# Query and key projections: the input's high and low parts moved through TensorE together

## The chip, the core and the metric

The kernel runs on one core of a Trainium2 chip. The metric is the time of one execution on the device in microseconds. Before the change it is 883.79 us, the median of three runs (883.66 to 884.83).

The core's engines work side by side, each through its own queue in order: TensorE (PE) multiplies matrices and writes its sums to PSUM, a memory of 8 banks of 128 partitions by 512 fp32; VectorE (DVE) and ScalarE (ACT) do elementwise work and can read PSUM; GpSimd (POOL) does elementwise work in SBUF; SyncE (SP) issues the loads of weights.

## The reference

A decoder trunk of two layers over 256 tokens of 1024 features, all in fp32. Each layer normalises its input, projects it, runs three attention mixers beside each other, gates and adds them, and then a feed-forward network. The parts around the change:

```python
    h = _rms_norm(x, attn_norm)
    proj = h @ w_in
    aq, ak, av, bq, bk, bv, c_q, c_kv_pe, gates = jnp.split(proj, offsets, axis=-1)
    ...
    y_a = _diff_attention(aq, ak, av, lam, lam_init, slopes_a, diff_norm) @ w_branch_a
    y_b = _dilated_attention(bq, bk, bv, slopes_b) @ w_branch_b
    y_c = _mla(c_q, c_kv_pe, mla_q_norm, mla_w_uq, mla_kv_norm, mla_w_ukv, pos) @ w_branch_c
```

The change is in the computation of `aq`, `ak`, `bq` and `bk`, 512 features each, in both layers.

## The kernel before

**Numbers in two parts.** The matmuls take numbers of a short format (`F32R`). Each fp32 operand is therefore split: ACT writes the rounded high part (`hi_of`, L222), DVE the remainder, the low part (`lo_of`, L225). A product is three matmuls, high by high, high by low and low by high, added in PSUM (`mm3`, L212).

**Weights.** A fixed list (`PLAN`) orders the pieces of all weights, each up to 128 x 1024. SP loads a piece into one of five `raw` tiles, ACT and DVE split it into one of five pairs `whi`/`wlo`, and `take` (L255) hands it out, after it has split the piece that lies three further on. A piece of a query or key projection holds four blocks of 128 inputs for 256 features, so one projection of 256 features takes two pieces.

**The input.** The normalised input lies transposed in tiles `fr`, as `self.xs`: for each of eight blocks of 128 features one run of 512 columns, the 256 tokens' high parts and then their low parts. The division by the root mean square comes after the projection: `Rb` (L421) is a row of one factor per token, repeated in all partitions and for two feature blocks.

**The projections.** `qk_proj` (L505) is called twice in a layer, for the first mixer (`stacked`) and for the second. A call makes four projections, j = 0 and 1 the queries, 2 and 3 the keys, each 256 features by 256 tokens. `pair_job` (L263) puts a projection into one bank: two halves of 128 features, each 256 columns, three matmuls per input block and half, with the weights standing and the input moving. DVE then reads the bank once, times `Rb` (queries also times the scale, L514; keys L516), into an `f` tile; the bank is returned, and the `f` tile is split again for the scores (`stacked` L491, `split` L232, `key_pair` L486).

**Banks.** Four banks form the ring `banks` for projections and the feed-forward network, four the ring `att` for attention. A bank that is returned goes to the end of its ring. While the latent projections of the third mixer wait for their factor, they hold two banks of the first ring. After the first `qk_proj` comes `mla_up` (L548), the query up-projection, with four banks: per block of 128 tokens two, 384 columns each.

**The order of work.** The generator `dense` (L455) yields after each piece; the attention's stages are called in between, 16 heads of three kinds (four of the first mixer, eight latent heads, four of the second) with fixed lags (L919 to L936). The program is built by a planner that simulates the engines' times (L1147) and sets the order of every engine's queue from that; so the order on the chip is fixed, and not always that of the source. In the first layer POOL also makes the mask tables (`tables`, L326) and in both it rotates the latent keys and queries (`rope`, L594).

Of the kernel before, what the change touches and what calls it, by code (L numbers as in the profile page):

```python
# [14 lines left out]
AF = mybir.ActivationFunctionType  # L15
ALU = mybir.AluOpType
# [163 lines left out]
def split_rows(t):  # L180
    return t.rearrange("p (c t) -> p c t", c=2)


class Build:
# [76 lines left out]
        return [(self.whi[j][:, k * nc_:(k + 1) * nc_], self.wlo[j][:, k * nc_:(k + 1) * nc_]) for k in range(nk)]  # L261

    def pair_job(self, ps, x, nk):  # L263
        k = 0
        while k < nk:
            for wh, wl in self.take():
                for c in range(2):
                    s = slice(c * 128, c * 128 + 128)
                    self.mm3(ps[:, c * 256:c * 256 + 256], wh[:, s], wl[:, s], x[k][:, 0:256], x[k][:, 256:512],
                             k == 0 and c == 0, k == nk - 1)  # L270
                k += 1
            if k < nk:
                yield
# [231 lines left out]
    def qk_proj(self, q, k, scale, stacked):  # L505
        nc = self.nc
        for j in range(4):
            bank = self.banks.get()
            yield from self.pair_job(bank, self.xs, KT)
            ps = split_rows(bank)  # L510
            t = self.f.get()
            tv = split_rows(t)
            if j < 2:
                nc.vector.scalar_tensor_tensor(out=tv, in0=ps, scalar=-scale, in1=self.Rb, op0=ALU.mult, op1=ALU.mult)  # L514
            else:
                nc.vector.tensor_tensor(out=tv, in0=ps, in1=self.Rb, op=ALU.mult)  # L516
            self.banks.put(bank)
            if stacked:
                (q if j < 2 else k).append(self.stacked(t, j < 2, j))
            elif j < 2:  # L520
                hi, lo = self.fr.get(), self.fr.get()
                self.split(hi, lo, t)
                q.append((hi, lo))
            else:
                k.append(self.key_pair(tv))
            self.f.put(t)
            yield
# [624 lines left out]
```

## Time and profile before

| | us |
|---|---|
| Median of three runs | 883.79 |
| The profiled execution | 883.18 |
| Its span, first to last instruction | 881.4 |
| PE busy | 873.6 |
| DVE busy | 591.1 |
| ACT busy | 502.2 |
| POOL busy | 71.4 |

The profile is one execution. Busy time is the time in which an engine has an instruction under way; matmuls overlap, so a busy PE may still have its instructions spaced out. In a row of a timeline the first two numbers are the start and the length in us from the span's start; `out<-in` are tiles, `xN` merges N like instructions, and a bracket at the end tells how long the engine was idle before it and who ended that. For a matmul the tile named first after the arrow is the one that moves.

### The profile page before, as it was taken

How to read it: one execution, taken by the hardware profiler on the slowest of the kernel's cores; microseconds unless marked ns; L12 is line 12 of the kernel's file. 1: busy time of each engine (PE TensorE's matmuls, PEld its weight loads, DVE VectorE, ACT ScalarE, POOL GpSimd, SP SyncE). 2: the span in 40 equal slices, each digit the busy share in tenths (PEclk: the TensorE clock that was granted, in tenths of full speed). 3: DMA queues.
4: the chain of work that ended last, by engine and by line, in shares of the span. 5: the costliest groups of instructions: out<-in, count | busy, mean ns of one | idle time of the engine just before them, and what ended most of it. 6: DMA issues, size and time to landing. Idle time of an engine off the chain costs nothing.

```text
span 881.4 us, 12736 instructions
## 1 busy us (share of the span) xinstructions
PE 873.6 (99%) x4710; PEld 759.5 (86%) x4710; DVE 591.1 (67%) x990; ACT 502.2 (57%) x852; POOL 71.4 (8%) x95
## 2 busy tenths in 40 slices
PE   9999999999999999999999999999999999999997
PEld 9989988888888888888899899888888888888886
DVE  5988878665666655555467888786556666656444
ACT  7797777644454444444376867775454644444332
POOL 1940310000000000000011303100000000000000
PEclk9999999999999999999999999999999999999999
DMA  9756444456656665656475553444555556655541
GB/s 340 245 170 209 128 141 160 146 169 193 187 167 197 187 190 182 182 186 191 127 226 174 172 168 128 151 145 159 180 189 182 167 193 202 203 190 180 181 141 49
DMA packets 45423, 155.92 MB, mean 177 GB/s; under 512 B 5168, under 2 KB 6192, under 8 KB 45360
## 3 DMA queue, kind: packets, MB, share of 16 engines
q1 hardware_dynamic: 44928, 154.55, 55.0%
q8 instruction: 37, 0.61, 0.3%
q10 hardware_dynamic: 432, 0.55, 0.2%
q14 instruction: 26, 0.21, 0.1%
HBM read 154.03 MB, written 1.05 MB: 176 GB/s over the span
## 4 chain that ended last, share of the span: by engine, by line
PE 97%; POOL 1%; issue 1%; DVE 0%; ACT 0%; POOLq 0%
PE bank L210 87%; PE att L210 6%; PE att L445 2%; PE att L719 1%; PE att L767 0%; PE att L768 0%; PE att L769 0%; POOL f L602 0%; PE att L693 0%; PE att L851 0%; POOL f L604 0%; POOL f L603 0%; POOL q_tm L605 0%; DVE x_tm L1043 0%; ACT x_tm L1058 0%
## 5 line engine op out<-in xcount | busy, mean ns | idle before, releaser
L210 PE MATMUL bank<-whi,fr 128*128 128x512 f32 (+1 forms) x2032 | 631.1, 387 | 0.0
L228 DVE TENSOR_TENSOR wlo<-raw,whi 128x1024 fp32r<-128x1024 f32 (+2 forms) x294 | 353.9, 1206 | 250.8 <-ACT whi L223 250.1
L223 ACT ACTIVATE whi<-raw 128x1024 fp32r<-128x1024 f32 (+2 forms) x294 | 305.0, 1041 | 305.8 <-PE bank L210 246.0
L210 PEld LDWEIGHTS bank<-whi,fr 128*128 128x128 f32 x2032 | 379.8, 188 | 71.5 <-ACT whi L223 0.2
L210 PE MATMUL bank<-wlo,fr 128*128 128x512 f32 (+1 forms) x1016 | 390.1, 386 | 0.0
L210 PEld LDWEIGHTS bank<-wlo,fr 128*128 128x128 f32 x1016 | 191.0, 188 | 35.5 <-DVE wlo L228 0.3
L210 PE MATMUL bank<-fr,whi 128*128 128x256 f32 x512 | 94.6, 285 | 0.0
L210 PEld LDWEIGHTS bank<-fr,whi 128*128 128x128 f32 x512 | 80.0, 192 | 0.2
L210 PE MATMUL bank<-fr,wlo 128*128 128x256 f32 x256 | 73.0, 285 | 0.0
L210 PEld LDWEIGHTS bank<-fr,wlo 128*128 128x128 f32 x256 | 49.0, 192 | 0.0
L372 POOL TENSOR_TENSOR r<-small,mhalf 128x2 f32<-128x2 f32 x4 | 2.8, 708 | 477.5 <-DVE small L398 462.6
L759 ACT ACTIVATE s<-s,small 128x256 f32<-128x256 f32 (+1 forms) x80 | 35.8, 455 | 1.2 <-DVE small L757 0.8
L372 POOL TENSOR_TENSOR small<-small,mhalf 128x2 f32<-128x2 f32 (+1 forms) x12 | 10.0, 831 | 280.5 <-DVE small L1047 178.5
L223 ACT ACTIVATE fr<-att 128x512 fp32r<-128x512 f32 (+2 forms) x54 | 28.3, 559 | 4.1 <-PE att L719 2.3
L210 PE MATMUL att<-whi,fr 128*128 128x288 f32 (+1 forms) x108 | 29.9, 290 | 0.0
L228 DVE TENSOR_TENSOR fr<-att,fr 128x512 fp32r<-128x512 f32 (+2 forms) x46 | 28.2, 634 | 0.1
L223 ACT ACTIVATE fr<-f 64x512 fp32r<-64x512 f32 (+2 forms) x40 | 23.3, 583 | 6.7 <-DVE f L516 5.4
L210 PE MATMUL att<-fr,fr 96*128 96x256 f32 (+3 forms) x152 | 26.0, 277 | 0.0
L210 PEld LDWEIGHTS att<-fr,fr 96*128 96x128 f32 (+1 forms) x152 | 22.7, 190 | 0.6
L615 ACT ACTIVATE f<-bank,rh 128x512 f32<-128x512 f32 x24 | 16.3, 689 | 11.7 <-PE bank L210 11.7
L972 ACT ACTIVATE f<-bank,rh 128x512 f32<-128x512 f32 (+1 forms) x24 | 15.6, 654 | 12.2 <-PE bank L210 12.2
L210 PEld LDWEIGHTS att<-whi,fr 128*128 128x128 f32 x108 | 20.4, 191 | 0.1
(134 smaller groups left out, 636.0 us busy)
## 6 DMA issues: line engine op xcount, KB each, us to landing
raw<-w SPq DMA_DIRECT2D x272, 512.0 KB, 3.6
raw<-w SPq DMA_DIRECT2D x16, 336.0 KB, 3.2
raw<-w SPq DMA_DIRECT2D x6, 384.0 KB, 3.6
x_tm<-xt SPq DMA_DIRECT2D x2, 512.0 KB, 6.4
f<-x SPq DMA_DIRECT2D x3, 256.0 KB, 5.2
f<-fnorm SPq DMA_DIRECT2D x2, 256.0 KB, 4.2
out<-x_tm ACTq DMA_DIRECT2D x2, 256.0 KB, 2.2
f<-x SPq DMA_DIRECT2D x2, 128.0 KB, 3.1
```

What stands on the lines that cost most here:

```text
L210: self.nc.tensor.matmul(out, lhsT, rhs, start=start, stop=stop, skip_group_check=True)
L223: self.nc.scalar.activation(out=hi, in_=src, func=AF.Copy, scale=scale)
L228: self.nc.vector.tensor_tensor(out=lo, in0=src, in1=h, op=ALU.subtract)
L372: self.nc.gpsimd.tensor_tensor(out=out, in0=v, in1=self.mhalf[:, 0:v.shape[1]], op=ALU.pow)
L445: self.nc.tensor.transpose(ps[:, c, b * 128:b * 128 + 128], src[b][:, c0 + c * 128:c0 + c * 128 + 128], self.ident)
L615: nc.scalar.activation(out=t[b], in_=bank[b], func=AF.Tanh, scale=self.rh[:, b:b + 1])
L719: nc.tensor.transpose(ps[0:96, c, b * 128:b * 128 + 128], src[:, b, 2 * p + c, :], self.ident)
L759: nc.scalar.activation(out=s[:, SL[b]], in_=s[:, SL[b]], func=AF.Exp, bias=mn[:, b:b + 1], scale=-1.0, accum_out=z[:, b:b + 1])
L972: nc.scalar.activation(out=a, in_=g, func=AF.Tanh, scale=self.rh[:, b:b + 1])
```

## The change

A projection now takes two banks, one for each half of 128 features. For an input block, the high weights meet the whole run of 512 columns, so that the products with the high and with the low part lie side by side in the bank; the low weights meet the 256 high columns. On reading, ACT copies the right half of a bank to the `f` tile, with the scale for queries, DVE adds the left half to it, and POOL multiplies both halves by `Rb`.

```diff
     def pair_job(self, ps, x, nk):
...
                 for c in range(2):
                     s = slice(c * 128, c * 128 + 128)
-                    self.mm3(ps[:, c * 256:c * 256 + 256], wh[:, s], wl[:, s], x[k][:, 0:256], x[k][:, 256:512],
-                             k == 0 and c == 0, k == nk - 1)
+                    self.mm(ps[c], wh[:, s], x[k], k == 0, False)
+                    self.mm(ps[c][:, 0:256], wl[:, s], x[k][:, 0:256], False, k == nk - 1)
                 k += 1
...
     def qk_proj(self, q, k, scale, stacked):
         nc = self.nc
         for j in range(4):
-            bank = self.banks.get()
+            bank = [self.banks.get() for _ in range(2)]
             yield from self.pair_job(bank, self.xs, KT)
-            ps = split_rows(bank)
             t = self.f.get()
             tv = split_rows(t)
-            if j < 2:
-                nc.vector.scalar_tensor_tensor(out=tv, in0=ps, scalar=-scale, in1=self.Rb, op0=ALU.mult, op1=ALU.mult)
-            else:
-                nc.vector.tensor_tensor(out=tv, in0=ps, in1=self.Rb, op=ALU.mult)
-            self.banks.put(bank)
+            sign = -scale if j < 2 else 1.0
+            for c in range(2):
+                nc.scalar.activation(out=tv[:, c], in_=bank[c][:, 256:512], func=AF.Copy, scale=sign)
+                nc.vector.scalar_tensor_tensor(out=tv[:, c], in0=bank[c][:, 0:256], scalar=sign, in1=tv[:, c],
+                                               op0=ALU.mult, op1=ALU.add)
+            self.banks.put(*bank)
+            nc.gpsimd.tensor_tensor(out=tv, in0=tv, in1=self.Rb, op=ALU.mult)
```

## Rows read from the trace of the kernel before

**Rows 1.** The page's head and busy table: us, share of the span, instructions.
```profile
span 881.4 us, 12736 instructions
...
PE 873.6 (99%) x4710; PEld 759.5 (86%) x4710; DVE 591.1 (67%) x990; ACT 502.2 (57%) x852; POOL 71.4 (8%) x95
```

**Rows 2.** The page's chain that ended last, shares of the span by engine.
```profile
PE 97%; POOL 1%; issue 1%; DVE 0%; ACT 0%; POOLq 0%
```

**Rows 3.** The page's groups, PE: busy us, mean ns, idle before.
```profile
L210 PE MATMUL bank<-fr,whi 128*128 128x256 f32 x512 | 94.6, 285 | 0.0
...
L210 PE MATMUL bank<-fr,wlo 128*128 128x256 f32 x256 | 73.0, 285 | 0.0
```

**Rows 4.** Pieces of the chain in order of time: start us, us, what.
```profile
82.35 2.87 PE bank L210 x24
...
283.29 21.79 PE bank L210 x96
```

**Rows 5.** Groups by line and shape, DVE, ACT and POOL; columns as in rows 3.
```profile
L514 DVE SCALAR_TENSOR_TENSOR f<-bank,row 128x512 f32<-128x512 f32 x8 | 5.5, 687 | 2.0 <-PE bank L210 1.9
...
L230 DVE SCALAR_TENSOR_TENSOR fr<-att,gains,fr 128x256 fp32r<-128x256 f32 x34 | 14.6, 477 | 0.4 <-ACT fr L223 0.3
...
L223 ACT ACTIVATE fr<-att,gains 128x256 fp32r<-128x256 f32 x34 | 13.8, 481 | 3.9 <-PE att L445 3.9
...
L602 POOL TENSOR_TENSOR f<-q_tm,cs 128x256 f32<-128x256 f32 x4 | 4.9, 1236 | 27.5 <-ACT q_tm L563 27.5
...
L605 POOL TENSOR_TENSOR q_tm<-f,f 128x256 f32<-128x256 f32 x4 | 2.9, 736 | 0.3
```

**Rows 6.** Busy us in stretches: length, PE, PEld, DVE, ACT, POOL, PEclk, DMA, GB/s.
```profile
34.00:40.00 6.00, 6.00 (x53) 6.00 (x52) 5.88 (x8) 4.03 (x6) 6.00 (x6) 1.00 0.77 254
40.00:46.00 6.00, 6.00 (x51) 6.00 (x50) 5.91 (x7) 1.35 (x3) 5.94 (x10) 1.00 0.55 180
...
474.00:480.00 6.00, 6.00 (x52) 6.00 (x52) 3.54 (x5) 4.42 (x6) 0.00 (x0) 1.00 0.52 178
...
87.00:102.00 15.00, 15.00 (x128) 14.91 (x127) 13.39 (x38) 11.55 (x34) 2.60 (x4) 1.00 0.39 108
```

**Rows 7.** Timeline of DVE, evacuations of keys and a weight split.
```profile
43.87 0.69 DVE L516 TENSOR_TENSOR f<-bank,row 128x512 f32<-128x512 f32 x1
...
47.23 0.69 DVE L516 TENSOR_TENSOR f<-bank,row 128x512 f32<-128x512 f32 x1
48.32 2.36 DVE L228 TENSOR_TENSOR wlo<-raw,whi 128x1024 fp32r<-128x1024 f32 x2 [0.39 <-ACT whi L223]
...
480.63 0.69 DVE L516 TENSOR_TENSOR f<-bank,row 128x512 f32<-128x512 f32 x1
```

**Rows 8.** Timeline of PE, first layer, from the query up-projection on.
```profile
45.38 0.52 PE L210 MATMUL bank<-whi,fr 128*128 128x384 f32 x2
...
51.62 0.28 PE L210 MATMUL att<-fr,fr 128*128 128x256 f32 x1
...
52.77 0.40 PE L210 MATMUL bank<-whi,fr 128*128 128x512 f32 x1
...
60.62 0.54 PE L719 MATMUL att<-ident,q_tm 128*96 128x128 f32 x3 [0.55 <-POOL q_tm L605]
```

**Rows 9.** Timeline of ACT, first layer, key split of j = 2 and weights.
```profile
44.60 2.60 ACT L223 ACTIVATE fr<-f 64x512 fp32r<-64x512 f32 x4 [4.73 <-DVE f L516]
47.22 2.01 ACT L223 ACTIVATE whi<-raw 128x1024 fp32r<-128x1024 f32 x2
```

**Rows 10.** Timeline of POOL, first layer: tables, key copies, query rotation.
```profile
24.23 4.49 POOL L338 TENSOR_SCALAR ta<-f 128x256 f32<-128x256 f32 x4
...
44.47 1.47 POOL L684 COPY k_tm<-kpe 128x256 f32<-128x256 f32 x2
52.86 0.75 POOL L602 TENSOR_TENSOR f<-q_tm,cs 128x256 f32<-128x256 f32 x1 [6.92 <-ACT q_tm L563]
...
56.21 1.72 POOL L602 TENSOR_TENSOR f<-q_tm,cs 128x256 f32<-128x256 f32 x1
```

## The prediction

> **What bounds the kernel now.** I read the page's busy table first. TensorE (PE) has 873.6 of 881.4 us with a matmul in flight [rows 1], but matmul ends are modelled and matmuls overlap, so this alone could hide waiting. So I went to the chain of waits, which follows the end of the run back from releaser to releaser: 97% of the span is PE [rows 2], and its pieces are long unbroken runs of matmuls. The reader is to see there that in most of the run nobody holds PE up: time is won by making PE's stream shorter, and lost only by making PE wait. The groups then say which matmuls the change touches: those in which the input (`fr`) moves, 512 against weights in `whi` and 256 against weights in `wlo`, all 256 columns wide [rows 3]. The code gives the same count: 4 projections a call (j = 0 to 3), 8 blocks of 128 inputs, 2 halves, 2 calls, 2 layers are 256 triples.
>
> **What a matmul costs in the stream.** The listed duration (285 ns) is a latency and overlaps its neighbours, so the price is the distance between starts. In the chain, 24 of these 256-column matmuls take 2.87 us: 119.6 ns each. In the feed-forward part, 96 matmuls of 512 columns take 21.79 us: 227.0 ns each [rows 4]. The clock is 1.00 in both layers' projections [rows 6]. 256 more columns cost 107.4 ns; a fixed 12.2 ns is left with every matmul, whatever its width.
>
> **The change on PE.** A triple of three 256-column matmuls is 358.8 ns. It becomes one of 512 (high weight against high and low input together) and one of 256: 346.6 ns. The columns are the same 768; one fixed share and one weight load go. Saved: 12.2 ns x 256 = 3.1 us, 0.78 us per call. All of it is on the path, since PE is the path. The weight load itself is hidden now (a 256-column matmul with a load of its own every 119.6 ns) and stays hidden behind a longer matmul. Bounds: 0 if the 512-wide form should cost two of 256; 3.3 us if the fixed share is the 12.9 ns that 119.6 leaves over 256 columns at 2.4 GHz. I take 3.1, from the two rows nearest to the forms used.
>
> The Trainium skill (TensorE: Matmul & The Clock Gate, Back-to-back issue gap) gives columns/2.4 plus 2.5 ns, and by it the change would be worth only 256 x 2.5 = 0.64 us, an estimate from that page; the trace does not agree here, with 12.2 ns per matmul in place of 2.5.
>
> **The change off PE.** Per projection one VectorE (DVE) pass of 0.687 us goes. In its place come two ScalarE (ACT) reads of 128x256 from PSUM, about 0.48 us each, two DVE passes of 128x256 about 0.48 us each, and one GpSimd (POOL) multiply of 128x512 [rows 5]. So DVE gains 0.27 us and ACT 0.96 us per projection, 16 projections in all. POOL's multiply has no row of its size. Below: twice the 0.736 us of the 128x256 addition L605, 1.5 us; above: twice the 1.72 us of the slowest 128x256 multiply [rows 5, 10], 3.4 us. I take 2.0, midway between twice 0.736 and twice the L602 mean of 1.236. The result reaches the splits after 0.48 + 0.48 + 0.48 + 2.0 = 3.4 us in place of 0.7.
>
> In three of the four calls this has cover. In the second layer's first call DVE is busy 3.54 of 6 us, POOL not at all [rows 6], and the evacuation starts as soon as the projection ends (480.63) [rows 7]. In both layers' second call the heads that need its results come after twelve other heads; DVE has 13.39 of 15 us there and ACT 11.55 [rows 6], and 4 projections over some 30 us add 1.1 and 3.8. If that cover went, PE would wait for split weights, but no row there shows PE doing so now. I put these three calls at 0.
>
> The first call in the first layer is tight. DVE has 5.88 and 5.91 of 6 us, POOL is full without a break from 24.23 to 45.94 with tables and key rotations, and only ACT has room (1.35 of 6 us in 40 to 46) [rows 6, 10]. Three queues matter:
>
> First, banks. There are four. A projection now holds two, so only one other projection lies between a bank's end and its next use, where three did. The query up-projection after it takes all four: its first 128 tokens those of projection j = 2, its second 128 those of j = 3. Today projection 2's evacuation starts at 43.87 and projection 3's at 47.23, ending at 47.92, 2.5 us after PE left it (45.38) [rows 7, 8]. DVE's queue grows by 4 x 0.27 = 1.1 us, so that lag becomes 3.6. PE can bridge it with the first half of the up-projection: its 36 matmuls run from 45.38 to 51.62, 173 ns each, so 18 are 3.1 us [rows 8]. PE then stands 0.5 us. Both ends: 0 if the planner lets the new evacuations pass the weight splits in DVE's order; 2 us if projection 2's banks are late as well.
>
> Second, ACT. It runs strictly in its order. Today it stands 4.73 us in front of the key split of projection 2, until DVE has evacuated it, and the weight splits of 47.22 are queued behind [rows 9]. With POOL in between that wait can grow by 2.7 us. Those weights are whole at 50.68 and first used at 52.77, and the second of the two pieces is needed later still [rows 7, 8]: 2.1 us of cover, and a planner that sees POOL's time puts the weight splits first. I take 0, with 2 as the upper end.
>
> Third, POOL. Four multiplies of 2.0 are 8 us. Between its last key copy and the query rotation POOL rests 6.92 us [rows 10]; the rest, 1.1 us, would push the rotation, for which PE already waits 0.55 us at 60.62 [rows 8]. But the 48 value matmuls (8 input blocks, 2 token blocks, 3 each; 10.9 us at 227.0) are ready behind that wait, and PE's order is laid out with the multiplies in view. I take 0.3; ends 0 and 7.
>
> The Trainium skill (SBUF — State Buffer, Who interferes with whom) says that a DVE instruction with two SBUF inputs contends with a GpSimd one that reads SBUF. The trace agrees in kind: the same multiply L602 took 0.75 us at 52.86 and 1.72 us at 56.21 [rows 10]. It speaks against this change, which puts POOL's reads where DVE is fullest, and is the mechanism of the slower rival below.
>
> **Sum.** 3.1 saved, 0.5 + 0.3 lost: 2.3 us less. The profiled execution took 883.18 us (span 881.4 and 1.78 around it), so 880.9. The median of the runs shown, 883.79, lies 0.61 above it: 881.5.
>
> **The rivals.**
> Rival A, the first layer takes most of it back: DVE's queue, two banks per projection and the ACT queue together hold PE by 1.4 to 4.9 us. For it: DVE is at 98% exactly there, and projection 2's evacuation already starts 4 us late (PE left it at about 39.6, one projection of 5.76 us before 45.38). Against it: PE has not one wait there now. At 3 us of waiting the time is 883.7, no change.
>
> Rival B, the matmul saves nothing: the 512-wide form with the input moving costs two of 256. For it: this kernel has no row of 512 moving input columns; today's 512-wide ones move weights. Against it: both are SBUF rows of 512 adjacent elements of one type. With the 0.8 us of losses: 884.6, or 883.9 when 0.7 is saved. This is also where the page's 2.5 ns would land.
>
> Rival C, slower: POOL in the first layer. Place: the four multiplies between 28 and 55 us, among table work that fills the queue, slowed by DVE. At 3.4 us each they are 13.8 us against 6.92 of rest: the query rotation is 6.9 us later, PE stands at the first latent head's transposes, and 6.9 + 0.5 - 3.1 = 4.3 us more: 888.1. It decides from the point where the multiplies add more than about 11.3 us (2.8 each) and the value matmuls are not put ahead: 11.3 - 6.9 + 0.5 = 4.9, which is the 3.1 saved and 1.8 on top. For it: 1.72 us for a half-size multiply. Against: 0.736 for the addition of that size, four times over, also beside a busy DVE.
>
> **How the numbers follow.** What a measurement of this kernel tells from no change is about 0.2%, 1.8 us. The forecast's case has chance 0.52: waits under 1.3 us, 880.6 to 882.0. Rival A 0.27 and rival B 0.06 both end within 0.2%. Rival C 0.15, from 885.6 upwards. So faster 0.52, same 0.33, slower 0.15. The range starts at 880.2 (nothing lost, 3.3 saved, and 0.3 of spread) and ends at 885.8, which leaves out most of C and little else.
>
> **What would show it.** Right: 256 matmuls fewer of `fr` against weights; 512-wide and 256-wide ones in pairs 347 ns apart from pair to pair; each of the three covered calls 0.8 us shorter, with no PE wait. The first layer's stretch to 61 us at most 0.8 us shorter, perhaps with a short PE wait around 48 us for DVE and a wait of about 0.9 us for the query rotation. Wrong: pairs at 359 ns (rival B); PE waits of several us for a bank, `whi` or `wlo` before 60 us (rival A); a long PE wait for `q_tm` with POOL multiplies of 3 us (rival C); or any PE wait in the second calls, whose cover I judged by the busy shares alone.

## The result and the profile after

The changed kernel takes 889.35 us (median of five, 889.15 to 890.24) against 883.79 us (five, 883.31 to 884.83): a ratio of 1.0062, with a 95% interval of 1.0049 to 1.0076. I had forecast 881.5 us, and the range ended at 885.8. It is 5.6 us slower where 2.3 us less were forecast.

First the page's head, busy table, chain and the groups of the change (busy us, mean ns, idle before), to be read against [rows 1 to 3, 5]:

```profile
span 887.4 us, 12277 instructions
...
PE 875.0 (99%) x4454; PEld 747.8 (84%) x4454; DVE 595.7 (67%) x1006; ACT 511.6 (58%) x884; POOL 85.8 (10%) x111
...
PE 90%; POOL 4%; ACT 2%; DMA 2%; issue 1%; DVE 1%; SPq 0%; POOLq 0%; ACTq 0%; DVEq 0%
...
L210 PE MATMUL bank<-fr,whi 128*128 128x512 f32 x256 | 92.1, 402 | 0.0
L210 PE MATMUL bank<-fr,wlo 128*128 128x256 f32 x256 | 71.3, 282 | 0.0
...
L519 POOL TENSOR_TENSOR f<-f,row 128x512 f32<-128x512 f32 x16 | 21.8, 1365 | 76.6 <-DVE f L516 72.7
```

The 256 matmuls are gone as said (4710 to 4454), and POOL's multiply is cheaper than I took it: 1.37 us, not 2.0. But PE's share of the chain falls from 97% to 90%; the difference goes to POOL, ACT and DMA. The list of what PE waited for (us in total, times, longest) says for whom:

```profile
PE att L721 <- POOL q_tm L607: 3.0, 2, 1.7
PE att L210 <- ACT fr L223: 2.0, 1, 2.0
PE bank L210 <- DVE ones L305: 1.0, 1, 1.0
```

The last of these stands in the kernel before too. The two waits for `q_tm` are one in each layer, so the second layer's first call, which I had put at nothing, lost as well.

**The first layer.** PE's timeline, to be read against [rows 8]; 384-column matmuls into `bank` are the query up-projection, L721 the transposes of the rotated queries:

```profile
43.26 0.40 PE L210 MATMUL bank<-fr,whi 128*128 128x512 f32 x1
...
44.64 0.51 PE L210 MATMUL bank<-whi,fr 128*128 128x384 f32 x2
...
47.42 0.51 PE L210 MATMUL bank<-whi,fr 128*128 128x384 f32 x2
49.93 0.50 PE L210 MATMUL att<-fr,fr 128*128 128x256 f32 x2 [2.00 <-ACT fr L223]
...
52.00 0.63 PE L210 MATMUL bank<-whi,fr 128*128 128x384 f32 x1
52.43 0.52 PE L210 MATMUL bank<-wlo,fr 128*128 128x384 f32 x1
...
54.67 0.38 PE L210 MATMUL bank<-whi,fr 128*128 128x384 f32 x1
...
66.18 0.53 PE L721 MATMUL att<-ident,q_tm 128*96 128x128 f32 x3 [1.32 <-POOL q_tm L607]
```

The up-projection starts at 44.64, which is 0.74 us earlier than before (45.38). The first call itself, from its first matmul to the up-projection's, takes 23.53 us in place of 24.23: its saving is there. The up-projection's first half (18 matmuls) is through at 47.9, and then PE stands 2.0 us. What ends that wait is another job, scores of the first mixer. The up-projection's second half begins only at 52.0. The transposes that stood at 60.62 stand at 66.18. Why the second half is late is to be read in ACT's and POOL's timelines (L515 copies the right half of a bank, L565 reads the query up-projection):

```profile
43.46 2.61 ACT L223 ACTIVATE fr<-f 64x512 fp32r<-64x512 f32 x4 [3.51 <-POOL f L519]
...
47.94 2.59 ACT L223 ACTIVATE fr<-f 64x512 fp32r<-64x512 f32 x4 [0.79 <-POOL f L519]
50.44 0.36 ACT L515 ACTIVATE f<-bank 128x256 f32<-128x256 f32 x1
50.82 1.06 ACT L223 ACTIVATE whi<-raw 128x1024 fp32r<-128x1024 f32 x1
51.79 0.36 ACT L515 ACTIVATE f<-bank 128x256 f32<-128x256 f32 x1
...
61.48 0.56 ACT L565 ACTIVATE q_tm<-bank,rq 128x384 f32<-128x384 f32 x1
```

```profile
42.13 2.54 POOL L519 TENSOR_TENSOR f<-f,row 128x512 f32<-128x512 f32 x2
44.63 0.70 POOL L607 TENSOR_TENSOR kpe<-f,f 128x32 f32<-128x32 f32 x1
45.40 0.81 POOL L686 COPY k_tm<-kpe 128x256 f32<-128x256 f32 x1
46.17 1.74 POOL L519 TENSOR_TENSOR f<-f,row 128x512 f32<-128x512 f32 x1
...
62.12 1.50 POOL L604 TENSOR_TENSOR f<-q_tm,cs 128x256 f32<-128x256 f32 x1 [5.44 <-ACT q_tm L565]
```

The last projection is complete when the up-projection starts (44.64), but ACT copies its halves only at 50.44 and 51.79. In ACT's queue they stand behind the key split of projection 2 (47.94), and that waits for POOL's multiply of 46.17, which in its turn stands behind rotations and copies of the latent keys. DVE adds the second half at 53.06 for 0.42 us, so the banks are free 8.8 us after the up-projection's start:

```profile
53.06 0.42 DVE L516 SCALAR_TENSOR_TENSOR f<-bank,f 128x256 f32<-128x256 f32 x1
```

In the kernel before it was 2.5 [rows 7, 8]. I call this the **release lag**. The up-projection's second 128 tokens need these two banks; its first 128 tokens keep PE busy for 3.1 us (the **bridge**), and the lag is now longer than that. So the last read of `q_tm` is late (61.48), POOL has stood still for 5.44 us when it comes, and PE waits for the rotation.

**The second layer.** Here POOL is empty, and still the same happens. Pieces of the chain that ended last (start, us, what):

```profile
482.07 1.30 POOL f L519
...
485.36 0.63 ACT fr L223
485.99 0.27 ACT f L515
...
486.28 1.07 ACT whi L223
...
487.37 1.23 DVE wlo L228
488.60 0.33 DVE f L516
...
497.04 0.47 ACT q_tm L565
...
500.23 1.60 POOL q_tm L607
...
501.87 0.53 PE att L721 x3
```

PE's timelines give the up-projection's start, here after the change (with the start of the pairs that the matmul saving is read from below) and then before it:

```profile
482.48 0.40 PE L210 MATMUL bank<-fr,whi 128*128 128x512 f32 x1
...
484.25 0.34 PE L210 MATMUL bank<-whi,fr 128*128 128x384 f32 x1
```

```profile
480.43 0.51 PE L210 MATMUL bank<-whi,fr 128*128 128x384 f32 x2
```

The up-projection starts at 484.25. Multiply, key split, and only then the copy of the last projection's first half; a weight split stands between this copy and the next; DVE ends at 488.93. The release lag is 4.7 us, where it was 0.9 (480.43 to the end of the evacuation at 481.32 [rows 7]), and at the end of the next stage PE waits 1.68 us for `q_tm`.

### The profile page after: what moved, and what is told of

It is laid out like the page before. It is cut to its first block, busy times and chain, and to the rows that moved or that the text cites. A ratio compares the mean times of both kernels' runs of the same rounds, so it can differ in the third digit from the quotient of the medians.

```text
span 887.4 us, 12277 instructions
## 1 busy us (share of the span) xinstructions
PE 875.0 (99%) x4454; PEld 747.8 (84%) x4454; DVE 595.7 (67%) x1006; ACT 511.6 (58%) x884; POOL 85.8 (10%) x111
## 4 chain that ended last, share of the span: by engine, by line
PE 90%; POOL 4%; ACT 2%; DMA 2%; issue 1%; DVE 1%; SPq 0%; POOLq 0%; ACTq 0%; DVEq 0%
PE bank L210 80%; PE att L210 5%; PE att L446 2%; DMA raw<-w 1%; PE att L721 1%; ACT fr L223 1%; DMA x_tm<-xt 1%; ACT whi L223 1%; POOL f L519 1%; POOL tb L343 1%; POOL tb L344 0%; PE att L769 0%; POOL ta L339 0%; PE att L770 0%; PE att L771 0%
## 5 line engine op out<-in xcount | busy, mean ns | idle before, releaser
L210 PE MATMUL bank<-fr,whi 128*128 128x512 f32 x256 | 92.1, 402 | 0.0
L210 PEld LDWEIGHTS bank<-fr,whi 128*128 128x128 f32 x256 | 47.8, 188 | 9.9
L519 POOL TENSOR_TENSOR f<-f,row 128x512 f32<-128x512 f32 x16 | 21.8, 1365 | 76.6 <-DVE f L516 72.7
L974 ACT ACTIVATE f<-bank,rh 128x512 f32<-128x512 f32 (+1 forms) x24 | 15.6, 654 | 12.2 <-PE bank L210 12.2
```

The source lines that it names most:

```text
L210: self.nc.tensor.matmul(out, lhsT, rhs, start=start, stop=stop, skip_group_check=True)
L519: nc.gpsimd.tensor_tensor(out=tv, in0=tv, in1=self.Rb, op=ALU.mult)
L974: nc.scalar.activation(out=a, in_=g, func=AF.Tanh, scale=self.rh[:, b:b + 1])
```

## The experiments

The first four runs (e1 to e4) were forecast under two theories: P, POOL's late multiply holds the splits and the banks; B, two banks per projection make the up-projection wait. The later ones were forecast under theory R (release), which came of the first four: the loss comes from the release lag of the last projection's banks, beyond the 3.1 us bridge; POOL and ACT matter as what makes the lag long. Its rival there is Q: every further step between the bank and the split costs by itself, whatever the banks. A last rival is a wide matmul that is dearer than thought. Times stand against runs of the kernel before on the same chip (medians 883.70 to 883.81).

| kernel | us | ratio (95%) | lag, us: layer 1, 2 | lost, us: layer 1, 2 |
|---|---|---|---|---|
| before | 883.79 | | 2.5, 0.9 | 1.3, 0.6 |
| after | 889.35 | 1.0062 (1.0049 to 1.0076) | 8.8, 4.7 | 6.8, 3.0 |
| e1 multiply on DVE | 886.63 | 1.0032 (1.0020 to 1.0045) | 6.9, 3.8 | 3.7, 2.6 |
| e2 multiply on POOL alone | 890.26 | 1.0076 (1.0064 to 1.0089) | 7.2, 0.9 | 6.7, 1.0 |
| e3 two banks alone | 884.29 | 1.0005 (0.9996 to 1.0014) | 3.4, 0.6 | 1.7, 0.7 |
| e4 second calls alone | 883.30 | 0.9993 (0.9985 to 1.0002) | 2.5, 0.9 | 1.3, 0.6 |
| e5 last projection as before | 885.37 | 1.0018 (1.0009 to 1.0026) | 6.3, 2.1 | 4.4, 0.8 |
| e7 the same, multiply on DVE | 884.01 | 1.0003 (0.9994 to 1.0012) | 3.8, 1.6 | 3.1, 0.8 |
| e8 DVE reads both halves | 887.73 | 1.0044 (1.0030 to 1.0058) | 6.0, 3.7 | 2.7, 3.6 |
| e13 splits behind copies | 886.42 | 1.0030 (1.0019 to 1.0041) | 7.5, 2.8 | 5.1, 0.8 |
| e14 the same, multiply on DVE | 884.17 | 1.0006 (0.9997 to 1.0015) | 5.1, 2.8 | 3.2, 1.0 |
| e17 other banks for the second half | 886.91 | 1.0033 (1.0021 to 1.0046) | 8.4, 4.3 | 6.4, 0.6 |
| e19 wide matmul bare | 883.02 | 0.9993 (0.9985 to 1.0002) | 3.7, 0.6 | 2.0, 0.7 |
| e20 wide where covered | 882.97 | 0.9994 (0.9985 to 1.0003) | 2.2, 2.1 | 1.0, 0.8 |

The lag is the end of DVE's last read of the last projection less the first 384-column matmul. "Lost" sums, from 1 us before that matmul to 25 us behind it, the distances between matmul starts less the steady price of their width (227, 173.5, 119.6 ns for 512, 384, 256 columns). Both are worked out from the profiled execution of each kernel. The 128-wide matmuls have no steady price here, so a sum is good to some 0.3 us.

**One part alone.**

e1, from the changed kernel:

```diff
-            nc.gpsimd.tensor_tensor(out=tv, in0=tv, in1=self.Rb, op=ALU.mult)
+            nc.vector.tensor_tensor(out=tv, in0=tv, in1=self.Rb, op=ALU.mult)
```

> The changed kernel, with the multiply by Rb on VectorE in place of GpSimd, all else as changed. Theory P (GpSimd's multiply, late behind the tables and followed by a strict ScalarE queue, holds the banks and the splits): the waits of 2.0 us before the scores, 1.3 and 1.7 us before q_tm go or fall below 0.5 each, the clock stays at 1.00, and the time is 881 to 883 us, since 3.1 us of matmul time are saved. Theory B (two banks for each projection, so that the query up-projection waits for the last key projection's banks): the waits stay within 1 us of what they are, and the time is 887 to 890 us.

886.63 us, between the two forecasts: 2.7 of the 5.6 us go, so P is only a part of it. The last copies still stand behind the key split, the lag stays above the bridge in both layers, and both lose.

e2, from the kernel before (its matmuls and its one bank; only the multiply moves to POOL):

```diff
-            if j < 2:
-                nc.vector.scalar_tensor_tensor(out=tv, in0=ps, scalar=-scale, in1=self.Rb, op0=ALU.mult, op1=ALU.mult)
-            else:
-                nc.vector.tensor_tensor(out=tv, in0=ps, in1=self.Rb, op=ALU.mult)
+            sign = -scale if j < 2 else 1.0
+            nc.vector.tensor_scalar(out=tv, in0=ps, scalar1=sign, scalar2=None, op0=ALU.mult)
+            nc.gpsimd.tensor_tensor(out=tv, in0=tv, in1=self.Rb, op=ALU.mult)
```

> The kernel before, with its three matmuls of 256 columns and one bank; only the evacuation is parted: VectorE scales the bank into the f tile and GpSimd multiplies it by Rb. Theory P: the same waits in the first layer come without any wide matmul, 886 to 890 us. Theory B: the banks come free as early as before, so 883.5 to 885 us.

890.26 us, 6.5 us slower without a single wide matmul or second bank, just above what P forecast and against B. By the table nearly all of it is in the first layer; with POOL empty in the second, next to nothing is lost there. ACT's list of waits in e2 shows the step:

```profile
ACT fr L223 <- POOL f L515: 18.1, 12, 4.4
```

The multiplies stand in POOL's full queue, the splits wait for them in ACT, and what stands behind the splits on ACT and DVE, the last projection's read among it, waits too.

e3, from the kernel before: three 256-column matmuls as before, but two banks per projection and two DVE passes:

```diff
...
+                    self.mm3(ps[c][:, 0:256], wh[:, s], wl[:, s], x[k][:, 0:256], x[k][:, 256:512], k == 0, k == nk - 1)
...
+                nc.vector.scalar_tensor_tensor(out=tv[:, c], in0=bank[c][:, 0:256], scalar=sign, in1=self.R,
+                                               op0=ALU.mult, op1=ALU.mult)
...
```

> The kernel before, with its three matmuls of 256 columns, each half of a projection in a bank of its own (left half of it), evacuated by two VectorE passes of 256 columns that multiply by the row as before; no GpSimd and no ScalarE pass. Theory B: the query up-projection is put behind the last projection's evacuation, waits of 2 us and more, 886 to 890 us. Theory P: 883.5 to 885 us.

884.29 us, not distinct from before, as P had it and against B. Two banks as such cost little; the lag of 3.4 us is about the bridge.

e4, from the changed kernel: the wide form in the second call of each layer only, the old form in the first:

```diff
-            bank = [self.banks.get() for _ in range(2)]
-            yield from self.pair_job(bank, self.xs, KT)
+            if not stacked:
+                bank = [self.banks.get() for _ in range(2)]
+                yield from self.wide_job(bank, self.xs, KT)
...
```

> The change in the second call of each layer (dilated attention) alone, the first call as before. Both theories: this call has 12 heads of cover, so 2 x 0.78 us are saved and nothing is lost: 882.0 to 882.6 us. If the busy shares misled me there, waits appear between 72 and 102 us and 506 and 536 us, and it is 883.5 or more.

883.30 us, 0.5 us less than the kernel before beside it, within the noise, and short of the 1.2 to 1.8 us that both theories forecast. No wait of PE stands in either second call, so they don't make the loss: it comes from the first calls.

**The lag, cut in several ways.**

e5 and e7, from the changed kernel, leave the last projection of the first calls (`stacked and j == 3`) in the old form, in one bank that DVE reads in one pass; e7 has the multiply of the other projections on DVE as well:

```diff
...
+            if not (stacked and j == 3):
+                bank = [self.banks.get() for _ in range(2)]
+                yield from self.wide_job(bank, self.xs, KT)
...
+            else:
+                bank = self.banks.get()
+                yield from self.pair_job(bank, self.xs, KT)
...
```

> The change, except that the last of the first call's four projections (j = 3) keeps the old form: three matmuls of 256 columns, one bank, one VectorE pass. GpSimd still multiplies the others. Theory R (the banks of j = 3 are released only by a ScalarE copy that stands in ScalarE's queue behind the split of j = 2, which waits for the multiply; the query up-projection needs those banks, and its rotation then comes late): the second layer's wait for q_tm (1.7 us) goes; in the first layer the split of j = 2 still waits for GpSimd, so part of the 5.5 us lost there stays; 884 to 887 us. Theory Q (each further step between the bank and the split costs by itself, whatever the banks): 888 to 890 us.

> As the run with one bank for the last projection, and the multiply by Rb on VectorE in place of GpSimd. Theory R: neither cause of the bank's late release is left; 882 to 883.5 us, at or below the kernel before, since three quarters of the first call and all of the second are wide. Theory Q: as the multiply on VectorE with two banks throughout, 886 to 887 us.

885.37 us, as R forecast, and 884.01 us, 0.5 above R's range and 2 below Q's. In the second layer the lag falls under the bridge and the loss goes (0.8). In the first layer e5 keeps a lag of 6.3 us; taking POOL out (e7) brings it to 3.8 and the time back to that of before.

e8, from the changed kernel, takes ACT and POOL out of the evacuation: DVE makes three passes.

```diff
-                nc.scalar.activation(out=tv[:, c], in_=bank[c][:, 256:512], func=AF.Copy, scale=sign)
+                nc.vector.tensor_scalar(out=tv[:, c], in0=bank[c][:, 256:512], scalar1=sign, scalar2=None, op0=ALU.mult)
...
-            nc.gpsimd.tensor_tensor(out=tv, in0=tv, in1=self.Rb, op=ALU.mult)
+            nc.vector.tensor_tensor(out=tv, in0=tv, in1=self.Rb, op=ALU.mult)
```

> The changed kernel with two banks throughout, but VectorE alone evacuates: it scales the right half into the f tile, adds the left half, multiplies by Rb. No ScalarE copy, no GpSimd. VectorE has about 1.8 us more work per projection than before. Theory R: the release no longer stands behind a split in ScalarE's queue; the second layer's first call loses under 0.5 us; the first layer, where VectorE was full, loses 1 to 3; 882.5 to 885.5 us. Theory Q: three passes in a row are as long a way as the change's, 886 us or more, with the second layer's loss of 2 us kept.

A miss for R, and what Q forecast: 887.73 us, and the second layer's loss stayed (3.6 us). DVE's timeline there, with the up-projection's start at 482.02:

```profile
482.86 0.75 DVE L515 TENSOR_SCALAR f<-bank 128x256 f32<-128x256 f32 x2
483.52 1.40 DVE L228 TENSOR_TENSOR low<-f,fr 64x512 fp32r<-64x512 f32 x2
484.95 0.76 DVE L516 SCALAR_TENSOR_TENSOR f<-bank,f 128x256 f32<-128x256 f32 x2
```

The first passes over the right halves come at once, but the adds stand behind the low parts of the key split. The banks are free at 485.71, 3.7 us after the start. So it is not ACT's queue as such: the last read can be late in whichever engine makes it. I had laid it too narrowly on ACT. The size of the loss does not follow the lag, though: 3.6 us were lost here with a lag of 3.7, and 3.0 after the change with one of 4.7. DVE has more work here, and whether that costs PE something by itself no run separates. The first layer lost more than the table's 2.7, too: a wait of 1.3 us for a bank inside the first call (at 39 us) lies ahead of its window.

e13, from the changed kernel, leaves every operation and ties the splits of a projection behind the copies of the next one:

```diff
...
-                nc.scalar.activation(out=tv[:, c], in_=bank[c][:, 256:512], func=AF.Copy, scale=sign)
+                read = nc.scalar.activation(out=tv[:, c], in_=bank[c][:, 256:512], func=AF.Copy, scale=sign)
...
+                with self.tc.issue_after(read.ins):
+                    for u, i in late + [(t, j)] * (j == 3):
+                        (q if i < 2 else k).append(self.stacked(u, i < 2, i))
+                        self.f.put(u)
+                late = [(t, j)]
...
```

> The changed kernel, two banks, ScalarE copies and GpSimd multiplies all kept; only ScalarE's order in the first call is tied: the splits of projection j are issued after the copies out of the banks of j + 1. Theory R: the up-projection's banks come free when the last projection ends; the second layer's 2.2 us of loss fall under 0.7 and the first layer's 5.5 under 4; 884.5 to 887 us. Theory Q: no step is shorter and the splits come later still; 889 to 892 us.

886.42 us, in R's range and under Q's: 2.9 of the 5.6 go by the order of the queue alone. In the second layer ACT now copies first and splits after; the lag is 2.8 us and the loss 0.8:

```profile
483.01 0.38 ACT L516 ACTIVATE f<-bank 128x256 f32<-128x256 f32 x1 [1.47 <-PE bank L210]
...
484.26 0.37 ACT L516 ACTIVATE f<-bank 128x256 f32<-128x256 f32 x1
484.53 2.59 ACT L223 ACTIVATE fr<-f 64x512 fp32r<-64x512 f32 x4
```

In the first layer it still loses 5.1 us, where R had said under 4. ACT copies in time (48.03, 49.23), but now DVE is late, as its timeline shows, and PE's wait names it:

```profile
44.95 4.53 DVE L228 TENSOR_TENSOR fr<-f,fr 64x512 fp32r<-64x512 f32 x4 [3.11 <-ACT fr L223]
...
50.74 0.41 DVE L517 SCALAR_TENSOR_TENSOR f<-bank,f 128x256 f32<-128x256 f32 x1
```

```profile
51.21 0.44 PE L210 MATMUL bank<-whi,fr 128*128 128x384 f32 x1 [2.75 <-DVE f L517]
```

The add stands behind the query splits' low parts and a weight split, and the query splits waited for ACT's high parts, which had waited for POOL:

```profile
44.28 1.29 ACT L223 ACTIVATE fr<-f 64x512 fp32r<-64x512 f32 x2 [3.80 <-POOL f L520]
```

e14 is e13 with the multiply on DVE:

> The changed kernel with ScalarE's order tied (splits of j behind the copies of j + 1) and the multiply by Rb on VectorE. Theory R with GpSimd as the first layer's part of it: the first layer's loss falls from 5.1 (tied alone) to 2 to 3.5, as in the run with one bank for the last projection and VectorE's multiply, and the second layer's stays at 0.75: 884 to 885.5 us. If GpSimd is not what delays the first layer: 886 to 887 us.

884.17 us, not distinct from before. With after, e1 and e13 it makes a square: the multiply's engine is worth 2.7 us in the one order (889.35 to 886.63) and 2.3 in the other (886.42 to 884.17), the order 2.9 and 2.5. The two together account for 5.2 of the 5.6 us. In the profiled executions TensorE's granted clock fell in the first layer after the change, but in none of the other three; some 1 us of the first step away from it, by either way, may be that (last section).

e17, from the changed kernel, leaves the lag and takes the need away: the up-projection's second half goes into two banks of the attention's ring.

```diff
-        pu = [[self.banks.get() for _ in range(2)] for _ in range(2)]
+        pu = [[ring.get() for _ in range(2)] for ring in (self.banks, self.att)]
...
-                self.banks.put(pu[b][f])
+                (self.banks, self.att)[b].put(pu[b][f])
```

> The changed kernel as it is; only the second half of the query up-projection takes its two banks from the ring att, so that it no longer uses the banks of the last projection. Theory R (PE's loss begins where the up-projection waits for those banks): the query rows are read as early as before, the second layer's loss falls from 3.0 us to under 1; in the first layer the split of j = 2 that waits for GpSimd still holds the scores, 2 to 4 us of 6.8 stay; 884.5 to 887 us. Theory Q (the way from the bank to the split is too long, whatever the banks): 888.5 to 890 us.

886.91 us, in R's range and under Q's. In the second layer the lag is still 4.3 us and the loss is gone (0.6): the strongest evidence for R, since nothing changed there but who needs the banks. The first layer is a miss for R: 6.4 us are lost, where 2 to 4 were forecast and 6.8 were lost after the change. The waits at 48 us and for `q_tm` go, but others come behind DVE, as the list of PE's waits in e17 shows:

```profile
PE att L210 <- DVE small L759: 1.2, 1, 1.2
PE bank L210 <- DVE f L516: 1.1, 1, 1.1
...
PE bank L210 <- DVE vc L230: 1.0, 1, 1.0
```

The second of these is the release lag once more: the next job (the latent keys and values) needs the same banks. The others are waits for DVE's work on scores and on a value split. And in this execution the clock fell, at 62.5 us, as the row of a stretch shows (columns as in [rows 6]):

```profile
63.00:64.00 1.00, 1.00 (x4) 0.81 (x3) 1.00 (x6) 1.00 (x2) 0.53 (x1) 0.50 0.74 156
```

Eight 512-column matmuls from 62.44 to 65.96 stand 440 ns apart where 227 is the steady price, some 1.7 of the 6.4 us.

**The matmul by itself.** e19 is e3 with the wide matmul; DVE reads the left half alone, so the product of the high weights with the low input is left out of the result:

```diff
-                    self.mm3(ps[c][:, 0:256], wh[:, s], wl[:, s], x[k][:, 0:256], x[k][:, 256:512], k == 0, k == nk - 1)
+                    self.mm(ps[c], wh[:, s], x[k], k == 0, False)
+                    self.mm(ps[c][:, 0:256], wl[:, s], x[k][:, 0:256], False, k == nk - 1)
```

> The wide matmul alone: two banks and matmuls of 512 and 256 columns as changed, but VectorE evacuates only the left half of each bank, times Rb, in two passes of 256, as in the run of two banks alone. The product of high weights and low input is left out of the result. By the spacing of the prediction (12.2 ns for each of 256 matmuls) this is 3.1 us under the two banks alone (884.3): 881.2 us. By the pairs of the changed kernel's trace (about 351 ns and some 87 ns at the start of a piece) it is 1.0 to 2.3 under: 882.0 to 883.3 us.

883.02 us, inside the range that the pairs gave: 0.7 under the kernel before beside it, where e3 was 0.5 above. That is 1.2 us for the matmuls, with some 1.1 of uncertainty from the two intervals. That leaves no room for 3.1.

e20 puts the change only where it loses nothing, in the second calls and in the second layer's first call without its last projection (`not stacked or (self.layer == 1 and j < 3)`):

> The change only where theory R finds no loss: the second call of both layers, and in the second layer's first call all but the last projection. The rest as before. Theory R: 0.5 us as measured for the second calls, and some 0.3 more: 882.8 to 883.5 us, below the kernel before by 0.3 to 1. If the second layer's first call loses by itself even with one bank for its last projection: 884 us or more.

882.97 us, 0.7 under before, in R's range, and its interval holds 1. No version here is clearly faster than the kernel before.

**What is shown, and what is not.** In the second layer three different edits (one bank for the last projection, another order of the same work, other banks for the next job) each take the loss away (e5, e13, e17), so the release lag is shown there. In the first layer the two parts are shown, POOL's place in the chain and the order of the splits and the reads. That they act through the up-projection's banks alone is not shown: e17 takes that need away and keeps most of the loss, since the lateness in ACT's and DVE's queues reaches PE by other ways as well.

## Why the prediction was wrong

**What failed.** The step is "In three of the four calls this has cover ... I put these three calls at 0", together with the bank term of the first call, "so that lag becomes 3.6". The first asked how busy the engines are, the second how much work DVE gains. Neither asked what stands ahead of the last read in the queue of the engine that makes it.
- *Second layer, first call.* I cited DVE at 3.54 of 6 us and an empty POOL [rows 6], and an evacuation that starts as soon as the projection ends [rows 7]. The shares stayed light after (DVE 4.03 of 6 us, POOL 2.03, ACT 3.28 in 474 to 480). But the copy stood behind a split that waits for the multiply, and the lag went from 0.9 to 4.7 us. It lost 2.4 us more than before; e13, e5 and e17 take that away in three ways.
- *First layer, banks.* I added 1.1 us of DVE work and came to 3.6; it was 8.8. Under "Second, ACT" I had the right queue ("It runs strictly in its order") and the right wait for POOL, but I looked only at the weight splits behind it, not at the new bank reads, which the change puts into that queue. The order came out the other way than the planner's care for POOL that I counted on.
- *POOL.* "I take 0.3; ends 0 and 7": moving the multiply alone to DVE gives 2.7 (e1) or 2.3 us (e14). It is not the multiply's price, which I had too high (1.37 us measured, under my lower end of 1.5). Its place in the full queue decides: projection 2's comes at 46.17, and the splits wait for it. Where else the first layer loses stays in part open (e17).

**What was mis-sized.** The matmul saving, 3.1 us. In the first call it nearly came true: 0.70 us less (0.78 forecast), and its last four pairs before 44.64 stand 345 ns apart. In the second layer the five pairs from 482.48 to 484.25 stand 354 apart, and over the undisturbed pairs (under 400 ns) the means of the four calls are 349 to 352, against 359 to 360 for a triple before: 8 to 11 ns in place of 12.2, 2.2 us in sum. Measured by itself (e19 against e3) the edit gave 1.2. Part of the rest may lie in the few slow pairs: single ones stand up to 433 ns apart, as triples of the kernel before do (up to 439), and with these counted the sum is 1.7 us. Where the remainder goes I can't say. The Trainium skill (TensorE: Matmul & The Clock Gate, Back-to-back issue gap) would put it, as an estimate, at 0.64 us by its 2.5 ns; e19 can't exclude that sum, but the pair distances show 8 to 11 ns.

**What held.** PE's stream is the time, and only waits lose. The second calls are covered (e4). Two banks as such are nearly free (e3). And the places to look were named: waits before 60 us and for `q_tm`.

**The rivals.** Rival C came nearest in time (888.1) and had the right layer for the larger part and the right victim, the query rotation. Its price was wrong (multiplies of 3.4 us; the longest was 2.03), and its 6.9 us of rest in POOL were not used up: 1.86 us of it were left when the first rotation began (53.17, before at 52.86). The late rotation is the second, and POOL stood still for 5.44 us ahead of it. Rival A had the mechanism, DVE's queue, two banks and ACT's queue together, but bounded it at 4.9 us and at one layer. Rival B fell: the pairs are not 360 apart. With 0.15 on C, and its start at 885.6, my range was too narrow on the slow side for a change that puts two more engines between a matmul and the return of its bank.

## What to carry to other kernels

When a read of PSUM moves to other engines, follow the bank and not the busy shares: from the last matmul through each queue to the return of the bank, with everything that stands ahead in these queues and what that waits for. Compare the sum with the work that PE can do without that bank (here 3.1 us); in the second layer lags below it cost next to nothing, and lags above it, where the banks were needed, cost 2 to 3 us at later places, though not in proportion. Put the reads that free a bank ahead of the work that uses their result, and keep a slow, full engine out of the chain between them.

## What the runs showed of the hardware

The granted clock fell in the first layer without being forecast. Stretches of the changed kernel (length, PE, PEld, DVE, ACT, POOL busy, PEclk, DMA share, GB/s):

```profile
48.00:49.00 1.00, 0.00 (x0) 0.00 (x0) 0.97 (x2) 0.98 (x2) 1.00 (x2) 1.00 0.00 0
...
51.00:52.00 1.00, 1.00 (x8) 1.00 (x8) 0.56 (x3) 1.00 (x2) 0.31 (x1) 0.67 0.69 274
52.00:53.00 1.00, 1.00 (x4) 1.00 (x5) 1.00 (x1) 1.00 (x3) 0.00 (x0) 0.50 0.58 234
...
55.00:56.00 1.00, 1.00 (x7) 0.87 (x6) 0.38 (x4) 1.00 (x5) 1.00 (x2) 1.00 0.94 381
```

PE stood from 47.9 to 49.9, ran at full clock for over 1 us, and was then at 0.50 (1.2 of 2.4 GHz) until past 54. Seven 384-column matmuls from 52.43 to 54.67 are 320 ns apart, where they are 173 [rows 8]: about 1 us of the loss. In e17 PE stood for 1.24 us to 59.91 and 0.96 us to 62.44, and was then at 0.50 until past 65. In e13 PE stood for 2.75 us (to 51.21), and in that execution the clock stayed at 1.00. What separates these cases no run here tells. Nor do the five times after the change show what the fall costs: the execution with the highest mean clock (0.998) took 889.65 us, more than the median.

POOL's 128x512 multiply took 1.29 us in the median and 2.03 at most after the change. 14 of the 16 took 1.30 us or less; the one that the key split of projection 2 waits for (46.17) took 1.74, all but 0.03 us of it beside a split on DVE. So it was slowed less than the 0.75 against 1.72 us of [rows 10] had made me fear.
